# Nearest-neighbour upsampling: x loaded in two DMAs instead of three, and the first store issued without a hold

## Chip, cores and metric

The kernel runs on one core of a Trainium2 chip; the other cores are not used by it. The metric is the device time of one execution in microseconds (us). Three executions of the kernel before took 197.62, 197.13 and 197.50 us, so its median is 197.5 us.

## What is computed

Every pixel of x becomes a block of scale_factor x scale_factor equal pixels of the result. The scale factor is 2.

```
x: (16, 64, 64, 64) float32, scale_factor = 2
result: (16, 64, 128, 128) float32
result[:, :, i, j] = x[:, :, i // 2, j // 2]
```

The input is 16.78 MB and the result 67.11 MB. There is no arithmetic: the work is to bring x into the on-chip memory, to write each row in its doubled form beside it, and to send that out.

## The kernel before, in words

**Layout.** All image rows of x, 16 x 64 x 64 of them, are dealt out to 128 partitions, so that each partition holds R = 512 consecutive rows of W = 64 floats (128 KB). A partition's share of the result is contiguous too: one input row becomes two output rows of 128 floats, 1 KB together. One tile, `mem` (line 187), has room for 20,224 floats per partition and behind them all of x (`xt`, line 188).

**Loads.** x comes in at line 194 by DMAs that SP issues. The cut points in line 192 make three: rows 0 to 255 (64 KB in each partition, 8192 KB in all), rows 256 to 479 (56 KB, 7168 KB) and rows 480 to 511 (8 KB, 1024 KB). A helper, `begin_before_barrier` (line 13), puts the first load ahead of the barrier that opens the program. All three are issued in the first 1.6 us. They are called load 0, load 1 and load 2 below.

**Chunks.** The loop at line 205 walks over nine chunks of rows, `rows = [52, 40, 52, 63, 52, 64, 63, 63, 63]`. For chunk n, VectorE (DVE) copies the first 9/16 of the rows into their doubled form (line 214) and ScalarE (ACT) the rest (line 215); then SP issues a store of the chunk (line 216), called store n below. Even chunks are built at the start of `mem`. Odd chunks are built so that they end where their own rows of x begin, which overwrites rows of x that were already used. So the copies of chunk n have to wait until the store of chunk n-2, which reads the same region, has landed. The copies of chunks 0 to 3 read rows of load 0 alone; chunk 4 (rows 207 to 258) is the first that needs load 1, and chunk 8 the only one that reads rows 480 to 511.

**What orders the work around the change.** Loads and stores are all issued by SP, in the order in which they stand in the program, and all go through one DMA queue (q1) to the 16 DMA engines. SP waits for the two copies of a chunk before it issues the chunk's store. On top of this, lines 217 to 225 make SP hold store 0 until `loads[-2]`, load 1, has landed. Store 1 stands behind store 0 on SP, so it is held as well. Load 2 is not waited for by the hold.

**The end.** `close_early` (line 80) rewrites the closing instructions so that only the last store's semaphore is waited for at the very end; the other landings are waited for by GpSimd. The change does not touch it.

Of the kernel before, what the change touches and what calls it, by code (L numbers as in the profile page):

```python
# [153 lines left out]
@with_exitstack  # L154
def kernel(
    ctx: ExitStack,
    tc: tile.TileContext,
    x: bass.AP,
    scale_factor: int,
    out: bass.AP,  # L160
):
    nc = tc.nc
    nc.at_finalize(begin_before_barrier)
    nc.at_finalize(close_early)
    P = nc.NUM_PARTITIONS
    s = int(scale_factor)
    B, C, H, W = x.shape
    R = B * C * H // P
    fdt = x.dtype

    xp = x.rearrange("b c h w -> (b c h) w").rearrange("(p r) w -> p r w", p=P)
    op = out.rearrange("b c (h hd) w -> (b c h) (hd w)", hd=s).rearrange(
        "(p r) w -> p r w", p=P
    )

    rows = [52, 40, 52, 63, 52, 64, 63, 63, 63]
    GROW = s * s
    FREE = 79
    WF = FREE * GROW * W
    assert sum(rows) == R
    mem_pool = ctx.enter_context(tc.tile_pool(name="mem", bufs=1))
    mem = mem_pool.tile([P, WF + R * W], fdt, name="mem")
    xt = mem[:, WF:].rearrange("p (r w) -> p r w", r=R)

    cuts = [0, R // 2, R - 32, R]
    loads = [
        nc.sync.dma_start(out=xt[:, lo:hi], in_=xp[:, lo:hi])
        for lo, hi in zip(cuts, cuts[1:])
    ]

    def expanded(r0, r1):
        return (
            xt[:, r0:r1].unsqueeze(2).unsqueeze(4).to_broadcast([P, r1 - r0, s, W, s])  # L200
        )

    r0 = 0
    before = (0, 0)
    for n, k in enumerate(rows):
        size = k * GROW * W
        at = 0 if n % 2 == 0 else WF + r0 * W - size
        assert at >= before[1] or at + size <= before[0]
        before = (at, at + size)
        u = mem[:, at : at + size].rearrange(  # L210
            "p (k a w b) -> p k a w b", k=k, a=s, w=W
        )
        kv = k * 9 // 16
        nc.vector.tensor_copy(out=u[:, :kv], in_=expanded(r0, r0 + kv))  # L214
        nc.scalar.copy(out=u[:, kv:], in_=expanded(r0 + kv, r0 + k))  # L215
        store = nc.sync.dma_start(out=op[:, r0 : r0 + k, :], in_=u)  # L216
        if n == 0:
            tc.add_manual_dep(
                store.ins,
                loads[-2].ins.name,  # L220
                mybir.DependencyInfo(
                    mybir.DependencyClass.Sync, mybir.DependencyReason.DATA
                ),
                reason="stores begin as the loads end",
            )
        r0 += k


# [33 lines left out]
```

## Time and profile before

| what | value | from |
|---|---|---|
| three executions | 197.62, 197.13, 197.50 us (median 197.5) | the times |
| span of the profiled execution, first to last instruction | 195.8 us | the page |
| median less span | 1.7 us | difference; the profiled execution's own time outside its span is not recorded |
| DMA queue q1 | 1728 packets, 83.89 MB, 99.3% of 16 engines' span | the page, part 3 |
| HBM read / written | 16.78 MB / 67.11 MB | the page |
| DVE, ACT busy | 69.6 us (36%), 51.4 us (26%) | the page, part 1 |
| load 0 landed | 21.8 us after its issue | issues of DMAs |
| load 1, load 2 landed | 38.0 us and 40.1 us after their issue | issues of DMAs |
| store 0 issued, landed | 38.86 us, 18.1 us later | chain of waits, issues of DMAs |
| SP held by load 1 ahead of store 0 | 37.2 us | waits of SP |

How to read it. The page has the busy share of each engine, a row of 40 slices of the span (a digit is the busy share in tenths), the DMA queues, the chain of work that ended last, and the groups of instructions. A DMA-issuing instruction is not busy time; the transfer itself shows only in the DMA rows. "Landing" is the moment when the last of the 16 DMA engines has reported. The trace also holds a record of every DMA packet with its start, length and size; each DMA here is 128 packets of one partition's row, eight for each of the 16 engines, and 16 tiny packets of 4 bytes that report the landing.

### The profile page before, as it was taken

Reading aid. Unit: us, or ns where it says so; the run is one execution under the profiler, and the core shown is the slowest. Engines: PE = TensorE matmul, PEld = TensorE weight load, DVE = VectorE, ACT = ScalarE, POOL = GpSimd, SP = SyncE. Lnnn points to the kernel's source line nnn. Section 1 sums busy time; section 2 is a strip of 40 time slices with the busy share of each in tenths; the row PEclk is TensorE's granted clock in tenths of the full one; section 3 lists DMA queues with packets and bytes.
Section 4 is the critical chain, followed back from the end, with each engine's and each line's share of the span. In section 5 each row is a group of like instructions: output and inputs, shape, how many; then the busy total and the mean of one; then the engine's idle time right before and its main releaser. Section 6 shows DMA issues by size and latency. Waiting matters only on the chain.

```text
span 195.8 us, 102 instructions
## 1 busy us (share of the span) xinstructions
DVE 69.6 (36%) x9; ACT 51.4 (26%) x10; POOL 0.2 (0%) x4
## 2 busy tenths in 40 slices
DVE  0000596000039289069007205930693079100000
ACT  2000558000036083064920005666000074000000
POOL 0000000000000000000000000000000000000000
DMA  9999889699899999999999899999999999999994
GB/s 428 428 428 428 375 375 562 288 462 522 348 442 410 513 402 468 402 422 422 422 422 522 348 522 428 428 428 428 422 422 422 422 422 435 474 488 488 435 422 211
DMA packets 1728, 83.89 MB, mean 428 GB/s; under 512 B 192, under 2 KB 192, under 8 KB 192
## 3 DMA queue, kind: packets, MB, share of 16 engines
q1 hardware_dynamic: 1728, 83.89, 99.3%
HBM read 16.78 MB, written 67.11 MB: 428 GB/s over the span
## 4 chain that ended last, share of the span: by engine, by line
DMA 67%; DVE 18%; issue 0%; DVEq 0%; SPq 0%
DMA out_dram<-mem 48%; DMA mem<-in_x_dram 19%; DVE mem L214 18%; DVEq L214 0%; SPq L216 0%
## 5 line engine op out<-in xcount | busy, mean ns | idle before, releaser
L214 DVE COPY mem<-mem 128x8960 f32<-128x8960 f32 (+3 forms) x9 | 69.6, 7738 | 97.8 <-DMA out_dram<-mem 75.9
L215 ACT COPY mem<-mem 128x7168 f32<-128x7168 f32 (+2 forms) x9 | 50.1, 5572 | 111.7 <-DMA out_dram<-mem 82.7
L215 ACT ACT_TABLE_LOAD x1 | 1.3, 1283 | 0.8 <-PEq L243 0.8
L243 POOL MEMSET const-bfloat16-1.0<- 128x1 bf16 x1 | 0.1, 101 | 0.0
L243 POOL MEMSET const-uint8-127<- 128x1 uint8 x1 | 0.1, 101 | 0.0
L243 POOL MEMSET const-float32-0.0<- 128x1 f32 x1 | 0.1, 98 | 0.2 <-issue 0.2
L243 POOL MEMSET const-float32-1.0<- 128x1 f32 x1 | 0.1, 98 | 0.0
## 6 DMA issues: line engine op xcount, KB each, us to landing
out_dram<-mem SPq DMA_DIRECT2D x4, 8064.0 KB, 28.4
out_dram<-mem SPq DMA_DIRECT2D x3, 6656.0 KB, 19.7
mem<-in_x_dram SPq DMA_DIRECT2D x1, 7168.0 KB, 38.0
out_dram<-mem SPq DMA_DIRECT2D x1, 5120.0 KB, 29.7
mem<-in_x_dram SPq DMA_DIRECT2D x1, 1024.0 KB, 40.1
mem<-in_x_dram SPq DMA_DIRECT2D x1, 21.8
out_dram<-mem SPq DMA_DIRECT2D x1, 29.9
```

The lines of the kernel that those rows point to most:

```text
L214: nc.vector.tensor_copy(out=u[:, :kv], in_=expanded(r0, r0 + kv))
L215: nc.scalar.copy(out=u[:, kv:], in_=expanded(r0 + kv, r0 + k))
L243: nc = _bacc.Bacc("TRN2", target_bir_lowering=False, num_devices=1)
```

## The change

The cut at row R - 32 goes, so that the former loads 1 and 2 become one DMA of 64 KB rows. The added dependency of store 0 goes. SP then issues store 0 as soon as chunk 0 is copied, and it stands in the queue behind the two loads; store 1 follows when chunk 1 is copied. In the built program SP has two load instructions instead of three, and nothing else moves on any engine. The other waits stay as they are; the semaphores of the DMAs are renumbered by one.

```diff
-    cuts = [0, R // 2, R - 32, R]
+    cuts = [0, R // 2, R]
     loads = [
         nc.sync.dma_start(out=xt[:, lo:hi], in_=xp[:, lo:hi])
         for lo, hi in zip(cuts, cuts[1:])
...
         nc.scalar.copy(out=u[:, kv:], in_=expanded(r0 + kv, r0 + k))
-        store = nc.sync.dma_start(out=op[:, r0 : r0 + k, :], in_=u)
-        if n == 0:
-            tc.add_manual_dep(
-                store.ins,
-                loads[-2].ins.name,
-                mybir.DependencyInfo(
-                    mybir.DependencyClass.Sync, mybir.DependencyReason.DATA
-                ),
-                reason="stores begin as the loads end",
-            )
+        nc.sync.dma_start(out=op[:, r0 : r0 + k, :], in_=u)
         r0 += k
```

## The prediction, made before the changed kernel ran

> **Forecast in one sentence.** The DMA engines are already busy without a gap from the first packet to the last, and the change takes about 0.06 us off what they have to do: 197.4 us, no change that can be measured. Here and below "no change" means within 0.3%, 0.6 us, about what a measurement of this kernel can tell from none.
>
> **What bounds the kernel now.** I read the page first, its slices and queue.
>
> ```profile
> ## 2 busy tenths in 40 slices
> DVE  0000596000039289069007205930693079100000
> ACT  2000558000036083064920005666000074000000
> POOL 0000000000000000000000000000000000000000
> DMA  9999889699899999999999899999999999999994
> ## 3 DMA queue, kind: packets, MB, share of 16 engines
> q1 hardware_dynamic: 1728, 83.89, 99.3%
> ```
>
> No engine but DMA is full. One digit invites a reading: the 6 in the eighth slice (34.3 to 39.2 us), just where the hold is. Read as a gap it would be 0.4 x 4.9 = 2.0 us of idle DMA, which the change might fill. So I took the windows, narrow around the switch from loads to stores, then wide.
>
> ```profile
> core 0: us, DVE busy (x) ACT busy (x) POOL busy (x), PEclk, DMA share, GB/s
> ...
> 36.00:37.00 1.00, 0.00 (x0) 0.00 (x0) 0.00 (x0) 1.00 1.32 573
> 37.00:38.00 1.00, 0.00 (x0) 0.00 (x0) 0.00 (x0) 1.00 0.06 25
> ```
>
> ```profile
> 3.00:21.00 18.00, 0.00 (x0) 0.00 (x0) 0.00 (x0) 1.00 0.95 411
> 21.00:34.00 13.00, 10.89 (x2) 9.13 (x2) 0.00 (x0) 1.00 1.08 468
> 34.00:43.00 9.00, 0.00 (x0) 0.00 (x0) 0.00 (x0) 1.00 1.02 440
> 43.00:57.00 14.00, 0.00 (x0) 0.00 (x1) 0.00 (x0) 1.00 0.95 412
> 57.00:65.00 8.00, 7.89 (x1) 5.10 (x1) 0.00 (x0) 1.00 0.95 410
> ```
>
> The column before the last is the DMA share. It is over 1 in one window and near 0 in the next: a window gets a packet whole, and a packet here lasts up to 2.4 us on all 16 engines almost in step. Over the 9 us from 34 to 43 the share is 1.02. The dip is the counting, not a gap. The trace's packet records say it exactly: with each packet cut at the edges of the window, 37 to 38 us is full as well, and no engine has over 0.03 us between one packet and the next anywhere from 1.0 to 195 us.
>
> The same records give the prices. The first packet begins at 1.01 us, the last ends at 195.45. The median packet of a size takes: 65,536 bytes 2.418 us, 57,344 bytes 2.116, 53,248 bytes 1.966, 8,192 bytes 0.309; the 4-byte reports take 0.009. Loads and stores of 64 KB take the same 2.418. Only the first data packet of each engine is longer, 3.20 in the mean. At 65,536 / 2.418 = 27.1 bytes per ns and engine, 16 engines move 434 GB/s, so 83.89 MB need 193.5 us. The span of 195.8 is this, 1.0 before the first packet, 0.8 in the long first packets, some 0.1 in fixed costs and skew, and 0.4 after the last. There is nearly nothing else in it.
>
> The chain of waits then has to be read with care. It puts 18% of the span on DVE, because a copy stands between two landings in it:
>
> ```profile
> 0.79 37.97 DMA mem<-in_x_dram
> 38.77 0.02 issue
> 38.78 0.03 SPq L216
> 38.81 0.05 issue
> 38.86 18.12 DMA out_dram<-mem
> 56.98 0.03 issue
> 57.00 0.02 DVEq L214
> 57.02 0.05 issue
> 57.07 7.90 DVE mem L214
> ```
>
> But while chunk 2 is copied, from 57 to 65 us, store 1 is running (DMA share 0.95 in that window). The queue is never empty there, so the copy costs nothing. Nor do the 38 us ahead of store 0's issue: the engines were loading.
>
> **Part 1: loads 1 and 2 become one.** Per engine, before: 8 x 2.116 + 8 x 0.309 = 19.400 us. After: 8 x 2.418 = 19.344, by load 0's packets, which have the same size and row pitch. That is 0.056 us less. One report per engine goes too, at most 0.009. SP issues one DMA less, 0.4 us on an engine that then waits anyway. Sum: -0.06 us on the path, since every packet is on the path. Could the 64 KB rows be worse than load 0's? All of load 0's packets but the first 16 took 2.42, so I put nothing on it.
>
> The rows up to 479 now land later. Load 1 landed at 38.77; the merged load lands when load 2 did, about 40.9 (its last packet ended at 40.85), 2.1 us later. The first reader is chunk 4, whose copies began at 84.8 when store 2 had landed. The cover is 44 us; only without it would the 2.1 us count.
>
> The Trainium skill has rules for both halves of this. "SBUF — State Buffer", in "The DMA setup-cost knee", charges each DMA about 2 us and says to coalesce; by it alone the merged load would save 2 us, 195.5. The trace says 0.06, since a queued DMA's fixed cost lies under its neighbour's packets. "Perfetto Trace Analysis", in "DMA Optimizations", speaks against the merge: splitting lets some work start sooner, if DMA engines are idle. By it the later landing would cost 2.1 us, 199.6; here no engine is idle and no reader is near.
>
> **Part 2: the hold goes.** Chunk 0's copies end at 21.86 + 5.10 (ACT) and 21.86 + 7.89 = 29.75 (DVE, mean row of this shape); chunk 1's at 33.87 (ACT, 29.84 + 4.03). So SP issues store 0 near 29.8 instead of 38.86 and store 1 near 33.9 instead of about 39.3. What does store 0 meet? It goes into the same queue as load 1, which has 8 packets per engine of which about half are left. Does it pass them? In the trace of before, store 0 was issued at 38.86; the first load took 1.01 us from issue to first packet, so by 39.9 store 0 could have started. Load 2's packets were 0.31 us each and went on beginning until 40.54; store 0's first packet began at 40.30, when the first engine had finished load 2, and the other engines followed by 40.85, each right behind its last load packet. Store 1, issued right behind store 0, moved no byte before 56.0. So the queue keeps order, and the stores' data moves when it moved before: store 0 from about 40.2 on, landed near 56.9. Everything behind it has the same distances as before, less 0.06 us.
>
> Does the longer queue cost anything? SP took 0.33 us for each store's issue and 0.33 to 0.42 for each load's, with up to three DMAs (1 MB per engine) outstanding at 1.6 us; at 34 us the rest of load 1 and stores 0 and 1 are about 0.2 + 0.43 + 0.33 = 0.96 MB. So SP shouldn't block, and if it did, nothing stands behind store 1 on SP before 65 us. Lower bound of this part: 0, as there is no gap to fill. Upper bound: the worst that packets did in this trace, see the second rival. I take 0, by the packets of 40.30 to 40.85, where some engines wrote and others still read: all had their usual length.
>
> Next late after a gain there would be nothing but the bytes. The margin of later stores stays: store 2 was issued at 65.0, while store 1 ran until 68.6.
>
> Sum: span 195.84 - 0.06 = 195.78; the median lies 1.7 above the span, which nothing here touches: 197.5 - 0.06 = 197.4.
>
> **Rivals.**
>
> 1. **No measurable change**, as worked out: 197.4. Within it is the case that dropping the hold does not do what it says: the store is issued 9 us earlier and its bytes move no earlier.
>
> 2. **Slower: queued stores disturb load 1.** Place: 30.8 us, a latency after store 0's issue, to the end of the load. If the engines serve a waiting store beside the load instead of behind it, reading and writing mix for the 10 us of load that are left, and about as many of store, 20 us in all. The order alone costs nothing, only slower packets do; it decides from 0.6 / 20 = 3% on. The only slow packets in the trace are the 16 first ones, 3.20 instead of 2.42, 32% and 0.78 us on each engine. If only the first mixed packet suffers so, +0.8: 198.2. If the turn back to stores alone costs as much again, +1.6: 199.0. If every packet of the mix did, 0.32 x 20 = +6.4: 203.8. Against it: the orderly 40.3 to 40.85 above. For it: no trace here shows a store waiting behind a load for 10 us. I take 198.2 as its time, by the row where a single packet is long.
>
> 3. **Faster: the 6 in the slices is a gap after all**, and early stores fill it: 197.5 - 2.0 = 195.5. Against it stand the share of 1.02 and the packet records. It would need executions without the profiler to have gaps that this one has not.
>
> **Chances.** First 0.69, second 0.27, third 0.04. Faster by over 0.3% is the third, 0.04; slower by over 0.3% the second, 0.27; the rest 0.69. The range runs from 196.9 (0.3% below) to 199.0, the second rival with two disturbed packets. Left out are the third case and that part of the second which I give 0.10, with a price beyond 1.6 us: 0.14.
>
> **What the new profile would show.** Right: store 0's issue near 29.8 and store 1's near 33.9; the merged load landing near 40.8; store 0 landing near 56.9, store 2 issued near 65.0; q1 with 1584 packets, still over 99%; a wide window over 34 to 43 still near 1.0; a span near 195.8. Wrong by the second rival: 53,248-byte packets beginning before 40 us, or load packets over 2.42 us after 30.8, and a later landing of store 0. Wrong by the third: a span under 195.2, with packets or gaps that shrank.

## The result, and the profile after

The changed kernel took 198.21 us (median of five, 198.11 to 198.60) against 197.24 for the kernel before (five, 197.13 to 197.62): 0.97 us more, ratio 1.0049 with a 95% interval of 1.0038 to 1.0060. The forecast was no change, 197.4. The time lies in the range; the sign was missed, and the end it took was the slower one. The profiled execution took 198.11 us with a span of 196.8; the span of before was 195.8, so the loss lies inside the span.

The page of the changed kernel: DMA row of the slices, the queue, and the bytes.

```profile
DMA  9999999988999997999999899999999999999994
...
q1 hardware_dynamic: 1584, 83.89, 99.2%
HBM read 16.78 MB, written 67.11 MB: 426 GB/s over the span
```

The 6 of the eighth slice is gone, as it was only the counting. The queue is as busy as before, 99.2% after 99.3%, with the same bytes. Only the rate fell, 428 to 426 GB/s: busy time grew. A full DMA row says that the engines have something in hand, not that they move it at their usual pace.

The chain of waits of the changed kernel, around the first store (start, length, what):

```profile
29.80 0.02 issue
29.82 0.02 SPq L216
29.84 0.05 issue
29.89 28.00 DMA out_dram<-mem
...
57.99 7.90 DVE mem L214
...
65.95 19.75 DMA out_dram<-mem
```

Store 0 was issued 9 us earlier and landed 0.9 us later, at 57.89 instead of 56.98. Store 2's issue moved from 65.0 to 65.95, and everything behind it is as late: the loss is complete before 58 us and is carried to the end unchanged.

The wide window over 34 to 43 us, which was expected near 1.0, shows a DMA share of 0.86 (column before the last):

```profile
34.00:43.00 9.00, 0.00 (x0) 0.00 (x0) 0.00 (x0) 1.00 0.86 328
```

That is no gap either: in the packet records every engine is busy through these 9 us, and a window counts a packet whole where it begins.

The packet records show where the time is lost. Load packets keep 2.42 us up to the eighth and last packet of load 1 on each engine, which begins near 38 us; that one took 3.07 to 3.68 us, 0.89 more in the mean of 16. The first store packet of an engine begins right after it, the earliest at 41.30 instead of 40.30. All store packets have their usual length. So the loss is 0.89 us per engine in the last packet of loading, while stores 0 and 1 stood in the queue. Below, "excess" is this: what an engine's load packets after 36 us took beyond the usual 2.418, 2.116, 0.611 or 0.309 us of their size, in the mean of the 16 engines. It is 0.00 in the kernel before.

### The profile page after: what moved, and what is told of

It reads as the page before. It is cut to its first block, busy times and chain, and to the rows that moved or that the text cites. A ratio compares the mean times of both kernels' runs of the same rounds, so it can differ in the third digit from the quotient of the medians.

```text
span 196.8 us, 100 instructions
## 1 busy us (share of the span) xinstructions
DVE 69.6 (35%) x9; ACT 51.4 (26%) x10; POOL 0.2 (0%) x4
## 3 DMA queue, kind: packets, MB, share of 16 engines
q1 hardware_dynamic: 1584, 83.89, 99.2%
## 4 chain that ended last, share of the span: by engine, by line
DMA 63%; DVE 22%; issue 0%; DVEq 0%; SPq 0%
DMA out_dram<-mem 52%; DVE mem L214 22%; DMA mem<-in_x_dram 11%; DVEq L214 0%; SPq L216 0%
```

## Experiments

Two theories were set against each other first: that the cost comes from the 64 KB packet at the end (L), or from a store that has stood in the queue (W).

**e1_no_hold**: the hold goes, the three loads stay. The edit against the kernel before ("..." stands for lines left out, here and below):

```diff
-        store = nc.sync.dma_start(out=op[:, r0 : r0 + k, :], in_=u)
-        if n == 0:
-            tc.add_manual_dep(
...
-            )
+        nc.sync.dma_start(out=op[:, r0 : r0 + k, :], in_=u)
```

> The kernel before without the hold, three loads kept. Two theories for the last load packet of each engine, which took about 3.31 us instead of 2.42 in the changed kernel. L (long packet): the cost belongs to a last load packet of 64 KB; 8 KB packets hide it. Then the eight 8 KB packets keep 0.31 us, span 195.8, ratio to before 1.000. W (waiting store): a store that has long stood in the queue makes the last load packet before it long, whatever its size. Then the last 8 KB packet of each engine takes about 1.2 us, span 196.7, ratio 1.0045.

Measured: 198.50 us, ratio 1.0062 (1.0040 to 1.0085), span 197.1, excess 1.15 us. Dropping the hold is enough for the loss; the merge of the loads is not needed for it. So L falls. W has the cause, but not the place: as load 2's packets are short, they show the course of the loss, and it is not the last packet that is long. On each engine up to three of the eight packets took 0.31 us, then about five took 0.34 to 0.77, and the last one or two 0.31 again. The first long ones began between 38.2 and 39.1 us, depending on the engine.

Windows show the same. First the kernel before, then this one (length of the window, busy us of DVE, ACT and POOL, clock, DMA share, GB/s):

```profile
38.00:39.00 1.00, 0.00 (x0) 0.00 (x0) 0.00 (x0) 1.00 0.95 401
39.00:40.00 1.00, 0.00 (x0) 0.00 (x0) 0.00 (x0) 1.00 1.04 442
```

```profile
38.00:39.00 1.00, 0.00 (x0) 0.00 (x0) 0.00 (x0) 1.00 1.11 352
39.00:40.00 1.00, 0.00 (x0) 0.00 (x0) 0.00 (x0) 1.00 1.03 229
40.00:41.00 1.00, 0.00 (x0) 0.00 (x0) 0.00 (x0) 1.00 0.81 197
```

Both have a DMA share near 1, but between 39 and 40 us the loads move 442 GB/s with the hold and 229 without: half the rate at full busy time.

**e2_late_store**: the changed kernel, with stores 0 and 1 made late by work on ScalarE. (Its second copy reads rows of x which chunk 1 has overwritten by then, so a part of chunk 0 in its result is not the reference's.)

```diff
+        if n == 0:
+            first = u
+        elif n == 1:
+            again = (first[:, 29:], expanded(29, 52))
+            nc.scalar.copy(out=again[0], in_=again[1])
+            nc.sync.dma_start(out=op[:, 0 : rows[0], :], in_=first)
...
```

> The changed kernel (two loads, no hold), with ScalarE's 5.1 us copy of chunk 0 done a second time after its copy of chunk 1, so that stores 0 and 1 are issued near 39.0 instead of 29.9 and 33.9; the last load packets would end by 40.3 to 40.9. L: last load packets still 3.3 us, span 196.7 to 196.8. W: last load packets near 2.42, span 195.8.

Measured: store 0 issued at 39.27; last load packets 2.42 us, excess 0.00, so L falls here as well. The span, 196.4, fits neither expectation, though. Engines waited 0.18 us in the mean between their last load packet and the first store packet, as the issue came 0.4 us later than in the kernel before; a further 0.43 us per engine is spread over the store packets from the first to the last, a few nanoseconds each, which none of the other runs shows and which I can't explain. Ratio 1.0017 (1.0007 to 1.0027).

**e4_hold_16k**: the hold stays, but the last load is 64 rows, which makes store 0 early.

```diff
-    cuts = [0, R // 2, R - 32, R]
+    cuts = [0, R // 2, R - 64, R]
```

> The kernel before with the hold, but the last load is 64 rows (16 KB packets, eight of 0.61 us per engine), so that store 0 is issued near 36.5, some 3 us before the last load packet of an engine begins. L: the excess of 0.89 us falls with the size, to at most a quarter, 0.2 us; span 195.8 to 196.0. W: about 0.9 us on the last 16 KB packet, span 196.7.

Measured: store 0 issued at 36.49, excess 1.11 us, span 197.1, ratio 1.0055 (1.0039 to 1.0071). W holds, with the correction of e1: it is not the last packet that is long but two or three before it, 0.8 to 1.4 us instead of 0.61, and the last one took 0.61 again on nearly every engine. The first long ones began between 37.9 and 39.1, depending on the engine. That is 1.4 to 2.6 us after the issue of store 0, but it is no latency: in e1 the store had been queued since 29.77, almost 7 us longer, and the long packets began at the same time. The place of the slow stretch goes by the end of the loads, not by the issue of the store.

What does the waiting store do? Its own packets come strictly behind the loads in all runs. Two theories: the engine already reads the store's data from the on-chip memory while it still writes load data into it (R, read ahead), or the store's writes to HBM disturb the reads from it (H). Two kernels put another kind of DMA behind the loads.

**x1_hbm_behind**: from HBM to HBM.

```diff
...
+            wide = xp[:, : k * GROW].rearrange("p (k a) w -> p k (a w)", a=GROW)
+            moved = nc.sync.dma_start(out=op[:, r0 : r0 + k, :], in_=wide)
...
```

> The kernel of e1_no_hold (three loads, no hold), but what stands behind the loads in place of store 0 is a DMA of the same size from x in HBM straight to chunk 0's part of the result, issued at the same time (so chunk 0 of the result holds x's first rows instead of its own). In e1_no_hold load 2's 8 KB packets took up to 0.69 us instead of 0.31, 1.15 us more per engine in all. R (read ahead): the engine reads the waiting store's data from the on-chip memory while it still writes load data into it; a waiting DMA that reads HBM does not do that. Load 2's packets stay near 0.31 us, excess under 0.2 us per engine. H (HBM): the waiting store's writes into HBM disturb the reads from it. Then this DMA disturbs too: excess of about 1.1 us per engine.

**x2_sbuf_behind**: from the on-chip memory into it.

```diff
+        if n == 1:
+            nc.sync.dma_start(out=u, in_=first[:, :k])
+            nc.sync.dma_start(out=op[:, 0 : rows[0], :], in_=first)
+            nc.sync.dma_start(out=op[:, r0 : r0 + k, :], in_=u)
...
```

> The kernel of e1_no_hold, but chunk 1 is not computed: behind the loads stands first a DMA of 40 KB rows from chunk 0's doubled rows to chunk 1's place in the on-chip memory, then store 0 and the store of chunk 1's place (so chunk 1 of the result holds chunk 0's rows). R: load 2's 8 KB packets are slow as in e1_no_hold, about 1.1 us excess per engine, as the waiting DMA reads the on-chip memory. H: no HBM is written by the first DMA behind the loads; packets near 0.31 us, excess under 0.2 us. The time is longer by the 12 us or more of the added DMA in both.

Measured, in one execution each: excess 0.00 us with the HBM copy, 1.29 with the on-chip copy. The same window in x1_hbm_behind, then in x2_sbuf_behind:

```profile
39.00:40.00 1.00, 1.00 (x1) 0.00 (x0) 0.00 (x0) 1.00 1.02 434
```

```profile
39.00:40.00 1.00, 0.00 (x0) 0.00 (x0) 0.00 (x0) 1.00 0.90 197
```

434 GB/s beside a waiting DMA that writes HBM but reads HBM, 197 beside one that reads the on-chip memory and writes no HBM. H falls. The HBM copy was issued at 27.1, 2.7 us before the store whose place it took in e1, so it had waited longer, not shorter. Store 1, which does read the on-chip memory, stood behind it from 34.0 on and cost the loads nothing either, so in this run only the DMA that came next could have counted, and it did not. (The whole times, 202.2 and 210.7 us, hold other things: the HBM copy ran slowly, the on-chip copy is added work.)

**e5_in_time** and **e6_bit_early**: the changed kernel's two loads, with stores 0 and 1 at two chosen times. ScalarE copies a part of chunk 0 onto itself, 21 or 17 rows.

```diff
+        if n == 0:
+            first = u
+        elif n == 1:
+            again = first[:, 29 : 29 + 21]
+            nc.scalar.copy(out=again, in_=again)
+            nc.sync.dma_start(out=op[:, 0 : rows[0], :], in_=first)
...
```

> The changed kernel's two loads without a hold, but ScalarE copies 21 rows of its part of chunk 0 onto themselves after chunk 1 (some 4.7 us), so that stores 0 and 1 are issued near 38.8, as in the kernel before. If only the time at which the store enters the queue matters: last load packets 2.42 us, span 195.8, ratio 0.9995 to 1.001. If 64 KB rows at the end cost something themselves: span up to 196.7.

> As e5_in_time with 17 rows (some 3.8 us), so stores 0 and 1 are issued near 37.9, 0.9 us earlier. R with a latency of 1.5 to 2.6 us from issue to the first disturbed packet, as seen in e4_hold_16k: reading ahead starts at 39.4 to 40.5 while loads end at 40.3 to 40.9: excess 0.2 to 0.6 us, span 196.0 to 196.4. If any waiting store costs its full price: span 196.7.

The chain of waits of e5_in_time, then of e6_bit_early:

```profile
33.89 4.58 ACT mem L220
38.47 0.02 issue
38.49 18.46 DMA out_dram<-mem
```

```profile
33.80 3.73 ACT mem L220
37.53 0.02 issue
37.54 20.02 DMA out_dram<-mem
```

Measured: e5 issued store 0 at 38.49, landed it at 56.95, excess 0.02, span 195.84, ratio 1.0005 (0.9996 to 1.0014): the two merged loads with a store in time are as fast as the kernel before. e6 issued it at 37.54, 0.95 us earlier: excess 0.65, a little above the expected 0.2 to 0.6, span 196.5, ratio 1.0047 (1.0030 to 1.0064). The full price of a waiting store is not met here, nor is it nothing: between 37.54 and 38.49 the price falls from 0.65 to 0.02. (The latency of 1.5 to 2.6 us that the expectation takes from e4 is not one, as said there.) The runs with store 0 issued whole, by the time of its issue:

| kernel | store 0 issued, us | excess, us | span, us |
|---|---|---|---|
| e1_no_hold | 29.77 | 1.15 | 197.1 |
| after | 29.89 | 0.89 | 196.8 |
| e4_hold_16k | 36.49 | 1.11 | 197.1 |
| e6_bit_early | 37.54 | 0.65 | 196.5 |
| e5_in_time | 38.49 | 0.02 | 195.8 |
| before | 38.86 | 0.00 | 195.8 |
| e2_late_store | 39.27 | 0.00, and 0.18 idle | 196.4 |

**f1 to f4**: if the price is that of the bytes read ahead, it must grow with the bytes that wait. In e5_in_time a piece of store 0, of one to four rows, is issued early; the rest follows in time.

```diff
             first = u
+            nc.sync.dma_start(out=op[:, 0:1, :], in_=u[:, :1])
...
-            nc.sync.dma_start(out=op[:, 0 : rows[0], :], in_=first)
+            nc.sync.dma_start(out=op[:, 1 : rows[0], :], in_=first[:, 1:])
```

> e5_in_time, with store 0 cut in two: its first row (1 KB in each partition, 8 KB for each DMA engine) is issued near 29.8 and waits behind load 1; the other rows follow in time as in e5. R with the price of the bytes read ahead: 8 KB / 27.1 bytes per ns = 0.3 us excess on the last load packets, span 196.1 to 196.2 (0.05 of it for the added DMA). If a waiting store costs its whole price whatever its size: 0.9 us excess, span 196.8.

> The same with two rows waiting, 16 KB for each DMA engine. By bytes read ahead: 0.6 us excess, span 196.4 to 196.5. Whole price: 0.9 us, 196.8.

> The same with four rows waiting, 32 KB for each DMA engine. By bytes read ahead: 1.2 us, if no limit comes first; a limit near 0.9 to 1.1 us (24 to 30 KB) is what the kernels with a whole store waiting would suggest. Span 196.8 to 197.1. Whole price: 0.9 us, 196.8.

> f1_rows_wait a second time. Its last load packets had only 0.06 us excess where the price of 8 KB read ahead would be 0.3. If that holds: 0.0 to 0.1 us again. If it was chance: about 0.3.

> Three rows waiting, 24 KB for each DMA engine. f2_rows_wait (16 KB) had 0.64 us and f4_rows_wait (32 KB) 0.98. By bytes alone, 0.9 us; a curve that starts only after the first 8 KB and levels off near 1.0 would give 0.8 to 0.9.

| waiting, KB per engine | excess, us | at 27.1 bytes per ns |
|---|---|---|
| 8 (f1_rows_wait) | 0.06 | 0.30 |
| 8 (f1_again) | 0.40 | 0.30 |
| 16 | 0.64 | 0.60 |
| 24 | 0.73 | 0.91 |
| 32 | 0.98 | 1.21 |
| 416 (the whole of store 0: after, e1, e4) | 0.89 to 1.15 | 15.7 |

Each row but the last is one execution. The price rises with the waiting bytes and levels off near 1 us, which at the packets' rate is some 27 KB per engine. That is no fixed price of a waiting store. The line by bytes is only roughly met: the two runs with 8 KB, the same kernel, lie on both sides of it and 0.34 us apart, as far as the rows with 16 and 32 KB. The spans, in the order of the table, were 196.4, 196.6, 196.6, 196.8 and 196.9. The first is longer than its excess says, and misses the 196.1 to 196.2 that was expected, because one engine ended its loads 0.7 us after the mean of the sixteen.

## Why the prediction failed

**What bounds the kernel: right.** The queue never empties, and any time lost by the engines is lost for the whole. So 0.89 us lost in one place appear almost unchanged in the median, as 0.97.

**Part 1, the merged load: right as far as it can be measured.** e5_in_time has the merged load and an in-time store, and its span is that of before. The 0.06 us are less than what the engines' first packets differ between executions (0.78 us excess before, 0.71 in e5). No reader waited for the later landing. That landing itself was misread: 40.9 is the end of the last packet, but the old load 2 landed at 1.17 + 40.1 = 41.3, and the merged one at 42.1.

**Part 2, order in the queue: right.** No store packet began before the engine's last load packet had ended.

**Part 2, "Does the longer queue cost anything?": wrong, and this is the step that failed.** It took 0 "by the packets of 40.30 to 40.85, where some engines wrote and others still read". The runs show 0.89 us in its place, on the last load packet of every engine, and 0.65 to 1.15 us in e1, e4 and e6. Those packets were no evidence, for two reasons. That some engines write HBM while others read it is not the case that matters; a store has to wait behind loads on one and the same engine. And store 0 was issued at 38.86, 1.4 to 2.0 us before the engines ended their loads, which is too late to cost anything: e5's store, issued 1.8 to 2.4 us before, cost 0.02, and e6's, 0.95 us earlier still, cost 0.65. The trace of before could not show the cost, because with the hold the store comes just late enough to escape it. The step should have taken this row for what it was, a store that came in time. That no trace showed a store waiting behind a load for 10 us was noted, under the second rival, and yet 0 was taken.

**The second rival: right time, wrong course.** 198.2 was priced with one long packet per engine, 0.78 us, taken from the start of the program, and one load packet that is 0.89 us longer is what the changed kernel showed. But the mix of 20 us that it described does not happen: no store packet passes a load packet. And with short packets it is not one that is long but about five (e1). The agreement of the numbers is partly luck. The sign to look for, load packets over 2.42 us and a later landing of store 0, was the right one.

**The third rival is out:** there was no gap to fill.

**What is shown, and what is argued.** Shown: load packets run at about half rate for 2 to 3 us shortly before the loads end (where the packets are short enough to tell, in e1, e4 and x2), if a DMA that reads the on-chip memory stands next in the queue early enough; not if it reads HBM (x1); not if it is issued 1.4 to 2.4 us before the end of the loads (e5, before). The price grows with the bytes that wait (f1 to f4, one execution each). Argued: that the engine reads these bytes ahead, and that these reads and the loads' writes share one path of 27 bytes per ns between an engine and the on-chip memory. No read is seen by itself in the records. The Trainium skill, "DMA: Bandwidth & Descriptors" in "Two DMAs through the same engine are not ordered", says that an engine's read and write sides are separate queues; that would let the read side go on to the store while the write side still has load data. The 229 GB/s at a DMA share of 1.03 agree with it, and so do the last load packets at full pace, if the engine reads only some 27 KB ahead. One thing it leaves open: in e2 the first store packet began 1.1 us after the issue. By that, the store of e5 could have begun at 39.6, about 1 us before the engines ended their loads, and yet it cost 0.02. Whether the shared path is a port of the memory or lies in the DMA engine wasn't tried, nor why a kernel with a whole store waiting has 0.89 in one case and 1.15 in another.

If such bytes are read ahead, they are not won back: the store packets that follow take as long as before, 1.97 us for each 53,248 bytes of store 0.

## What to carry to other kernels

On a queue that is never empty, an earlier issue brought nothing here and cost something: a store queued long behind loads took 0.9 to 1.15 us from them. The best time to issue it was 1.4 to 2.4 us before the loads' end (before, e5), when it neither disturbed them nor left a gap. A hold that looks idle in the waits of the issuing engine may be doing just that, so ask what the held DMA would do to its neighbours, and don't take a trace with the hold for evidence of the case without it. And read GB/s beside the busy share: the loss stood in the one and not in the other.

## What was unexpected of the hardware

- A DMA that reads the on-chip memory and waits next behind loads on one queue slows them before it moves a byte by the records: loads at 197 to 229 GB/s instead of 434 to 442 for 2 to 3 us, up to 1.29 us in all (x2_sbuf_behind).
- An issue that comes too late costs as well: at 39.27 instead of 38.86 the engines stood idle for 0.18 us in the mean (e2_late_store).
- The DMA from HBM to HBM in x1_hbm_behind took 4.4 us per engine more than a store of the same size: eight packets of 53,248 bytes with 2.52 us each in the mean instead of 1.97.
